# Queue order of early operands, loads from POOL's queue and a pause of preparing steps around the gate/up stage of a hybrid block

## The chip, the cores and the metric

The kernel runs on one core of a Trainium2 chip: TensorE (PE) for matrix products, VectorE (DVE), ScalarE (ACT), GpSimd (POOL), and SyncE (SP), which here only issues DMAs. The metric is device microseconds of one execution, smaller is better; the time given is the median of several runs.

## The reference

One layer on `x` of shape (1, 2048, 1024), all in float32. The part behind the two mixers is what matters here:

```python
mixed = jnp.concatenate([rmsnorm(y_ssm, norm_ssm_out_g[l]),
                         rmsnorm(y_att, norm_att_out_g[l])], axis=-1)
x = x + mixed @ w_out[l]
h2 = rmsnorm(x, norm_ffn_g[l])
x = x + (jax.nn.silu(h2 @ w_gate[l]) * (h2 @ w_up[l])) @ w_down[l]
...
return rmsnorm(x, norm_final_g)
```

The hidden width of the feed-forward part is `D_FF` = 2816. Ahead of it stand an input projection, a diagonal state-space mixer and chunked attention, which this change doesn't touch.

## The kernel before

**Products.** A float32 operand is split in two parts of a shorter type: `split` (L173 to L175) has ACT cast the high part and DVE subtract it from the value, which leaves the low part. `mm3` (L167, its matmuls on L79) makes three matmuls of each product: high times high, high times low, low times high. Nearly everything that PE does behind the attention reads such pairs, so each operand needs a DMA, an ACT cast and a DVE subtract first.

**Stages.** After the mixers (to about 900 us) comes the output projection: `w_out(sb, b, i)` for four blocks of 512 tokens and four pairs of 128-row tiles each. One call loads two tiles of `x` (`xt`, L1214), makes the products into the two-bank PSUM tile `big`, adds (L1222), stores the result as `x1` (L1223), squares it in place on ACT (L1228) and adds the squares into `sa` (L1229, L1230). The square writes where the store reads, so it waits until the store has landed. `xt` has two buffers.

Gate and up (`gate_up_phase`, about 922 to 1771 us) and down (`down_phase`, about 1771 to 2185 us) use a scheme with seven products in place of eight for a two-by-two block product; the seven are called B11, B21, T2, T1, T3, B22, T4 (numbers 0 to 6), and each reads sums or differences of blocks that were prepared before. A tail of norms and of the last tokens ends the program.

**Gate and up.** Two halves `hf` of the tokens, eleven blocks `f` of hidden rows in each, and for every block one `Proj` for gate and one for up. `one` makes B11 and T1, `two` makes T2, B21 and T3, and `three`, which is called inside the next `Proj`, makes B22 (into bank `Y`), adds, and makes T4 (into bank `X`). `product` splits the weights (`c`); the token operands of a half are seven pairs of tiles `hi`/`lo` of 1 MB each, loaded from `hc` and split by `build` (L1457). `EARLY` lists the five of them that are loaded while the output projection still runs, in the order B11, T1, T2, B21, T3; `LATE` holds B22 and T4:

```python
B11, B21, T2, T1, T3, B22, T4 = range(7)
EARLY, LATE = (B11, T1, T2, B21, T3), (B22, T4)
```

So `EARLY[:3]` are the tiles `lo0`, `lo3`, `lo2`, and `EARLY[3:]` are `lo1` and `lo4`. The first half's operands go as four loads each, the second half's as one load of 1 MB each. Between the `Proj`s, `next(pre, None)` takes one step of a generator: first the second half's token sums (`pre_steps`), then the down weights' sums (`weight_steps`, DVE adds on L1382 to L1390, results stored as `wc`).

**Down.** Hidden blocks in groups of three or two (`group`). A group makes the seven products in the order B11, T1, T2, B22, T3, B21, T4, each with an operand of hidden values from `hq` and one of weights from `wc`. `operand` takes a tile `hd` from a ring of ten, loads it (L1619) and splits it; for the first group, `early` has the loads issued by POOL, and those of B11 and T1 are issued at high priority. The results are added from PSUM (`ps`) into `acc` (L1653), which `load_acc` (L1658) fills from `x1` by 32 loads of 256 KB for the first group of each half.

**Order.** The program is given to a framework that fixes the order of each engine's instructions when the kernel is built: it takes them by priority (program order, or ahead of it inside `tc.high_priority()`), and by when it reckons that their inputs are ready. PE's order is kept as it is written. `tc.issue_after(ins)` makes what is issued inside it stand behind `ins` on the same engine. Each engine then runs its instructions strictly in that order. SP's DMAs take eight semaphores in turn, so a DMA is issued only when the one eight places before it has landed.

Of the kernel before, what the change touches and what calls it, by code (L numbers as in the profile page):

```python
# [12 lines left out]
AF = mybir.ActivationFunctionType  # L13
# [3 lines left out]
P = 128  # L17
# [80 lines left out]
def f32(ap):  # L98
    return ap.bitcast(F32)
# [73 lines left out]
def split(k, hi, lo, raw):  # L173
    nc = k.nc
    return nc.scalar.copy(hi, raw), nc.vector.tensor_tensor(lo, raw, f32(hi), op=ALU.subtract)  # L175
# [896 lines left out]
def mix_phase(k, S, bank):  # L1072
# [3 lines left out]
    with ExitStack() as cx:  # L1076
# [130 lines left out]
        def w_out(sb, b, i):  # L1207
            ts = slice(sb * SB, (sb + 1) * SB)
            if i == 0:
                b.sa = k.t(k.mf, "sa", [P, SB], bufs=2)  # L1210
            rows = slice(i * P, (i + 2) * P)
            xt = k.t(wr, "xt", [P, 1024], bufs=2)
            xv = xt[:].rearrange("p (q t) -> p q t", q=2)
            nc.sync.dma_start(xv, io["xt"][rows, ts].rearrange("(q p) t -> p q t", p=P))  # L1214
# [7 lines left out]
            nc.vector.tensor_tensor(xt[:], xt[:], ps[:], op=ALU.add)  # L1222
            nc.sync.dma_start(S["x1"][rows, ts].rearrange("(q p) t -> p q t", p=P), xv)  # L1223
            if i == 0:
                nc.scalar.activation(b.sa[:], xt[:, :512], AF.Square)
                nc.scalar.activation(xt[:, 512:], xt[:, 512:], AF.Square)
            else:
                nc.scalar.activation(xt[:], xt[:], AF.Square)  # L1228
                nc.vector.tensor_tensor(b.sa[:], b.sa[:], xt[:, :512], op=ALU.add)  # L1229
            nc.vector.tensor_tensor(b.sa[:], b.sa[:], xt[:, 512:], op=ALU.add)  # L1230
            yield

        def next_block(sb):
# [66 lines left out]
        for sb in range(NSB):  # L1300
            if sb:
                b.m = {}
                mixed(b, 0)
            if sb == 0:
                held = [w_out(0, b, 2 * n) for n in range(3)]
                next(held[0])
                next(held[1])
                ps = big()
                spread(k, te, ps[:, :512], b.o[1], 0)
                with tc.high_priority():  # L1310
                    rstd2(b, 1, ps[:, :512])
                    mixed(b, 1)
                next(held[2])
            else:
                mixed(b, 1)
            for n in range(4):
                if n == 0 and 0 < sb < NSB - 1:
                    nxt = next_block(sb + 1)
                if sb or n > 2:
                    for _ in w_out(sb, b, 2 * n):  # L1320
                        pass
                else:
                    next(held[n])
                if n in (0, 1) and xr:
                    next(xr)
                if n in (1, 2) and sb + 1 < NSB:
                    norm(nxt, n - 1)
                for _ in range(PRE0.get((sb, n), 0)):
                    next(pre)
                if (sb, n) == (NSB - 1, 1):  # L1330
                    rx.close()
                    k.ga1 = tc.alloc_tile_pool(name="ga1", reuse_waits="tile", bufs=1, side="right")
                    k.gr = tc.alloc_tile_pool(name="gr", reuse_waits="tile", bufs=2, side="right")
                    wr = cx.enter_context(tc.tile_pool(name="wr2", reuse_waits="tile", bufs=2, side="right"))
                    k.hT = build(k, S, 0, k.ga1, EARLY)
# [114 lines left out]
def build(k, S, hf, pool, ns):  # L1450

    hT = {}
    for n in ns:
        hi, lo = hT[n] = tuple(k.t(pool, f"{m}{n}", [P, 4, 512], F32R) for m in ("hi", "lo"))
        with k.tc.high_priority():
            for q in range(4) if hf == 0 else (slice(0, 4),):
                k.nc.sync.dma_start(f32(lo[:, q]), S["hc"][hf, n, :, q])  # L1457
        for q in range(4):
            split(k, hi[:, q], lo[:, q], f32(lo[:, q]))
    return hT  # L1460


def gate_up_phase(k, S):
# [3 lines left out]
    with ExitStack() as cx:  # L1467
# [13 lines left out]
        class Proj:  # L1481
# [49 lines left out]
                u3 = self.keep(self.x)  # L1531
                self.add(u3, self.y, 1, 1)

            def three(self):
                self.product(B22, self.s4, self.y, False)
                self.add(self.u2, self.y, 0, 1)
                self.product(T4, self.a22, self.x, False)
                self.post(self.x, 1, 0)

        before = None  # L1540
# [2 lines left out]
        for hf in range(2):  # L1543
            hT = build(k, S, 1, k.ga1, EARLY) if hf else k.hT
            hT.update(build(k, S, hf, ga, LATE))
            for f in range(F2):
                gs = {}

                def gt():
                    return k.t(gb, "g", [P, 512], bufs=GB_)  # L1550

                def gate(u, r, c, gs=gs):
                    g = gs[r, c] = gt()
                    nc.scalar.activation(g[:], u[:], AF.Silu)

                def up(u, r, c, gs=gs, hf=hf, f=f):
                    g = gs[r, c]
                    V.tensor_tensor(g[:], g[:], u[:], op=ALU.mult)
                    if hf and f + r * F2 in TAILF:
                        nc.sync.dma_start(S["h"][TAILF.index(f + r * F2), :, c * 512 : (c + 1) * 512], g[:])  # L1560
                        return

                    def put(n, b):
                        nc.sync.dma_start(S["hq"][hf, f, n], b[:])

                    if (r, c) == (0, 0):
                        put(B11, g)
                    elif (r, c) == (1, 1):
                        put(B22, g)
                    elif (r, c) == (0, 1):  # L1570
                        t1, t2 = gt(), gt()
                        V.tensor_tensor(t1[:], g[:], gs[0, 0][:], op=ALU.subtract)
                        put(T1, t1)
                        V.tensor_tensor(t2[:], gs[1, 1][:], t1[:], op=ALU.subtract)
                        put(T2, t2)
                        V.tensor_tensor(g[:], gs[1, 1][:], g[:], op=ALU.subtract)
                        put(T3, g)
                        gs["t2"] = t2
                    else:
                        put(B21, g)  # L1580
                        t4 = gt()
                        V.tensor_tensor(t4[:], g[:], gs["t2"][:], op=ALU.subtract)
                        put(T4, t4)

                for w, post in (("w_gate", gate), ("w_up", up)):
                    p = Proj(hT, io[w], f, post)
                    p.one()
                    if before:
                        before.three()
                    p.two()  # L1590
                    before = p
                    if hf or f > 1:
                        next(pre, None)
                if hf == 0 and f < 2:
                    next(xr)
        before.three()
    k.gr.release()
    k.ga1.release()

# [1 line left out]
def down_phase(k, S):  # L1601
    tc, nc, io = k.tc, k.nc, k.io
    V, te = nc.vector, k.te
    with ExitStack() as cx:
# [5 lines left out]
        def bank(pool):  # L1610
            return k.t(pool, "ps", [P, 512])

        def operand(src, early=False, aside=False):

            g, n = src.shape[0], src.shape[2]
            t = k.t(next(ring), "hd", [P, 2 * DG * 512], F32R)
            hi, lo = (t[:, m * g * n : (m + 1) * g * n].rearrange("p (g c) -> p g c", g=g) for m in range(2))
            with tc.high_priority() if early else ExitStack():
                (nc.gpsimd if aside else nc.sync).dma_start(f32(lo), src.rearrange("g p c -> p g c"))  # L1619
            split(k, hi, lo, f32(lo))  # L1620
            return hi, lo

        def group(hf, f0, g, acc, early):
# [6 lines left out]
            def load(m):  # L1630
                if m < len(order):
                    n = order[m][0]
                    soon = early and n in (B11, T1)
                    ops[n] = operand(S["hq"][hf, fs, n], soon, early), operand(S["wc"][fs, n], soon, early)

            if f0 == 0:
                acc += [k.t((a0, a1)[hf], f"acc{i}", [P, HALF]) for i in range(KT)]
# [241 lines left out]
```

## Time and profile before

| what | value |
|---|---|
| time, median of 3 runs | 2221.88 us (2221.82 to 2222.04) |
| profiled execution | 2217.26 us, span 2215.1 us |
| granted TensorE clock, mean | 0.992 |
| PE busy | 2153.9 us (97%) |
| DVE busy | 1534.0 us (69%) |
| ACT busy | 1009.9 us (46%) |
| POOL busy | 372.8 us (17%) |
| DMA | 431.20 MB, mean 195 GB/s |

Times in the rows below are microseconds from the start of the span. A row of the time line gives start, busy time, engine, line, operation, output and input, how many instructions stand in it, and in brackets how long the engine had idled before it and what it had waited for. A row of waits gives the total, how often, and the longest. A row of a stretch gives its bounds and length, the busy time of PE, of PE's weight loads, DVE, ACT and POOL, then the granted clock of PE, the share of the DMA engines in use and GB/s. A row of DMA issues ends with KB each and the median us from issue to landing.

### The profile page before, as it was taken

Reading aid. Unit: us, or ns where it says so; the run is one execution under the profiler, and the core shown is the slowest. Engines: PE = TensorE matmul, PEld = TensorE weight load, DVE = VectorE, ACT = ScalarE, POOL = GpSimd, SP = SyncE. Lnnn points to the kernel's source line nnn. Section 1 sums busy time; section 2 is a strip of 40 time slices with the busy share of each in tenths; the row PEclk is TensorE's granted clock in tenths of the full one; section 3 lists DMA queues with packets and bytes.
Section 4 is the critical chain, followed back from the end, with each engine's and each line's share of the span. In section 5 each row is a group of like instructions: output and inputs, shape, how many; then the busy total and the mean of one; then the engine's idle time right before and its main releaser. Section 6 shows DMA issues by size and latency. Waiting matters only on the chain.

```text
span 2215.1 us, 30093 instructions
## 1 busy us (share of the span) xinstructions
PE 2153.9 (97%) x10606; PEld 1817.4 (82%) x10606; DVE 1534.0 (69%) x2671; ACT 1009.9 (46%) x1681; POOL 372.8 (17%) x838
## 2 busy tenths in 40 slices
PE   8988999999989999999999999999999999999998
PEld 7777798998977888788888887888888778888887
DVE  8756566565568667767776768767666477689785
ACT  6356566555586631543333335333333443354332
POOL 3357777676210000000000000000000010000000
PEclk9999999999999999999999999999999999999999
DMA  9778977665743346835655557546333395465562
GB/s 331 232 246 282 298 227 235 210 208 155 224 129 127 118 143 200 277 100 186 189 160 197 196 190 269 200 158 209 114 100 114 112 393 181 169 219 199 188 221 77
DMA packets 194503, 431.20 MB, mean 195 GB/s; under 512 B 19760, under 2 KB 37216, under 8 KB 187248
## 3 DMA queue, kind: packets, MB, share of 16 engines
q1 hardware_dynamic: 186608, 404.31, 55.2%
q0 software_dynamic: 7744, 24.97, 3.6%
q8 instruction: 83, 1.36, 0.2%
q14 instruction: 68, 0.56, 0.1%
HBM read 290.00 MB, written 131.10 MB: 190 GB/s over the span
## 4 chain that ended last, share of the span: by engine, by line
PE 82%; DVE 8%; DMA 6%; issue 3%; ACT 2%; SPq 0%; POOL 0%; ACTq 0%; DVEq 0%
PE X L79 20%; PE ps L79 19%; PE pf L79 10%; PE Y L79 10%; PE big L79 6%; PE W L79 5%; PE pj L79 5%; PE pt L82 2%; PE sc L79 2%; DMA lo<-hc 1%; DMA hd<-wc 1%; DMA x<-xt 1%; DVE lo L175 1%; DMA xt<-in_xt 1%; DVE ptl L955 1%
## 5 line engine op out<-in xcount | busy, mean ns | idle before, releaser
L79 PE MATMUL X<-hi,c 128*128 128x512 f32 x1408 | 450.3, 390 | 7.6 <-DVE xt L1222 3.5
L79 PE MATMUL ps<-hd,hd 128*128 128x512 f32 (+1 forms) x1920 | 428.7, 384 | 2.6 <-DVE hd L175 2.0
L79 PEld LDWEIGHTS ps<-hd,hd 128*128 128x128 f32 x1920 | 353.2, 188 | 74.4 <-DVE hd L175 2.7
L79 PEld LDWEIGHTS X<-hi,c 128*128 128x128 f32 x1408 | 264.7, 188 | 64.4 <-DVE c L175 4.6
L79 PE MATMUL X<-lo,c 128*128 128x512 f32 x704 | 274.4, 390 | 0.0
L175 ACT CAST hd<-hd 128x1536 fp32r<-128x1536 f32 (+1 forms) x106 | 147.5, 1394 | 229.8 <-DMA hd<-hq 171.9
L79 PE MATMUL Y<-hi,c 128*128 128x512 f32 x704 | 224.5, 389 | 2.3 <-DVE u L1515 2.3
L175 DVE TENSOR_TENSOR hd<-hd 128x1536 fp32r<-128x1536 f32 (+1 forms) x106 | 174.3, 1646 | 37.0 <-ACT hd L175 36.4
L1619 POOL DMA_DIRECT2D hd<-hq x7 | 5.3, 757 | 1108.8 <-PE X L79 1095.0
L175 DVE TENSOR_TENSOR c<-S,c 128x512 fp32r<-128x512 f32 x176 | 121.1, 689 | 99.4 <-ACT c L175 99.1
L1511 ACT COPY u<-X 128x512 f32<-128x512 f32 x132 | 77.5, 588 | 195.0 <-PE X L79 195.0
L175 ACT CAST c<-S 128x512 fp32r<-128x512 f32 x176 | 109.5, 622 | 121.1 <-PE Y L79 61.6
L79 PE MATMUL big<-m,woh 128*128 128x512 f32 x512 | 161.3, 397 | 0.0
L79 PEld LDWEIGHTS Y<-hi,c 128*128 128x128 f32 x704 | 132.1, 188 | 30.6 <-DVE u L1515 3.2
L1653 DVE TENSOR_TENSOR acc<-acc,ps 128x512 f32<-128x512 f32 x196 | 130.5, 685 | 37.7 <-PE ps L79 37.3
L79 PEld LDWEIGHTS X<-lo,c 128*128 128x128 f32 x704 | 132.6, 188 | 27.5
L175 ACT CAST c<-raw 128x512 fp32r<-128x512 f32 x132 | 82.2, 623 | 148.1 <-PE Y L79 70.6
L79 PE MATMUL pf<-hi,w 128*128 128x512 f32 x416 | 147.7, 407 | 0.6 <-ACT hi L806 0.6
L79 PE MATMUL Y<-lo,c 128*128 128x512 f32 x352 | 137.0, 389 | 0.0
L955 DVE TENSOR_TENSOR ptl<-pt,pth 128x640 fp32r<-128x640 f32 (+3 forms) x152 | 98.2, 646 | 46.0 <-ACT pth L954 43.9
L938 ACT ACTIVATE s<-s,mn 128x640 f32<-128x640 f32 (+4 forms) x128 | 97.9, 765 | 53.6 <-DVE mn L935 52.0
L954 ACT CAST pth<-pt 128x640 fp32r<-128x640 f32 (+3 forms) x152 | 83.8, 551 | 77.0 <-PE pt L82 72.6
(479 smaller groups left out, 4293.6 us busy)
## 6 DMA issues: line engine op xcount, KB each, us to landing
w<-wss SPq DMA_DIRECT2D x36, 1024.0 KB, 6.0
hq<-g SPq DMA_DIRECT2D x140, 256.0 KB, 2.1
hd<-hq SPq DMA_DIRECT2D x35, 768.0 KB, 4.4
hd<-wc SPq DMA_DIRECT2D x35, 768.0 KB, 6.0
raw<-in_w_gate SPq DMA_DIRECT2D x44, 512.0 KB, 3.6
raw<-in_w_up SPq DMA_DIRECT2D x44, 512.0 KB, 4.1
wc<-px SPq DMA_DIRECT2D x66, 256.0 KB, 3.0
wss<-w SPq DMA_DIRECT2D x12, 1024.0 KB, 6.1
```

Source lines behind the costliest of these rows:

```text
L79: return self.tc.keep_in_program_order(self.tc.nc.tensor.matmul(*a, **b))
L82: return self.tc.keep_in_program_order(self.tc.nc.tensor.transpose(*a, **b))
L175: return nc.scalar.copy(hi, raw), nc.vector.tensor_tensor(lo, raw, f32(hi), op=ALU.subtract)
L938: nc.scalar.activation(s[:, :nk], s[:, :nk], AF.Exp, bias=mn[:], scale=-1.0, accum_out=sums[sb, pr][:, hh, qp : qp + 1])
L954: nc.scalar.copy(pth[:, a:b, qp, :], pt[:, a:b, :])
L955: nc.vector.tensor_tensor(ptl[:, a:b, qp, :], pt[:, a:b, :], f32(pth[:, a:b, qp, :]), op=ALU.subtract)
L1511: nc.scalar.copy(u[:], ps[:])
L1619: (nc.gpsimd if aside else nc.sync).dma_start(f32(lo), src.rearrange("g p c -> p g c"))
L1653: V.tensor_tensor(a, a, ps[:], op=ALU.add)
```

## The change

Six edits in four places:

1. `w_out` notes its last store, square and sum in `k.marks`. `build` for the first half is called twice: with `EARLY[:3]` as before, and with `EARLY[3:]` inside `issue_after` for those three marks. Eight loads (`lo1`, `lo4`) on SP, their casts on ACT and their subtracts on DVE come to stand behind the store, square and sum of the output projection's tile that was the latest at that point.
2. The second half's seven operand loads are issued by POOL, not by SP.
3. The last `Proj` makes T4 ahead of B22 (`three(True)`).
4. No step of the preparing generator is taken at the first half's last block and at the second half's first block (four calls of `next` fewer there).
5. The first down group's B11 operands are split, too, at high priority (`ahead`).
6. As a consequence of the new order, ACT loads its table for the square root (L1754, now L1768) ahead of the last `Silu`, and two more table loads follow.

```diff
-            nc.sync.dma_start(S["x1"][rows, ts].rearrange("(q p) t -> p q t", p=P), xv)
+            put = nc.sync.dma_start(S["x1"][rows, ts].rearrange("(q p) t -> p q t", p=P), xv)
...
-                nc.scalar.activation(xt[:], xt[:], AF.Square)
+                sq = nc.scalar.activation(xt[:], xt[:], AF.Square)
...
-            nc.vector.tensor_tensor(b.sa[:], b.sa[:], xt[:, 512:], op=ALU.add)
+            sa = nc.vector.tensor_tensor(b.sa[:], b.sa[:], xt[:, 512:], op=ALU.add)
+            k.marks = put, sq, sa
...
-                    k.hT = build(k, S, 0, k.ga1, EARLY)
+                    k.hT = build(k, S, 0, k.ga1, EARLY[:3])
+                    with ExitStack() as behind:
+                        for ins in k.marks:
+                            behind.enter_context(tc.issue_after(ins.ins))
+                        k.hT.update(build(k, S, 0, k.ga1, EARLY[3:]))
...
-                k.nc.sync.dma_start(f32(lo[:, q]), S["hc"][hf, n, :, q])
+                (k.nc.gpsimd if hf else k.nc.sync).dma_start(f32(lo[:, q]), S["hc"][hf, n, :, q])
...
-            def three(self):
+            def fourth(self):
+                self.product(T4, self.a22, self.x, False)
+
+            def three(self, last=False):
+                if last:
+                    self.fourth()
                 self.product(B22, self.s4, self.y, False)
                 self.add(self.u2, self.y, 0, 1)
-                self.product(T4, self.a22, self.x, False)
+                if not last:
+                    self.fourth()
                 self.post(self.x, 1, 0)
...
-                    if hf or f > 1:
+                    if 1 < hf * F2 + f not in (F2 - 1, F2):
                         next(pre, None)
...
-        before.three()
+        before.three(True)
...
-        def operand(src, early=False, aside=False):
+        def operand(src, early=False, aside=False, ahead=False):
...
-            split(k, hi, lo, f32(lo))
+                if ahead:
+                    split(k, hi, lo, f32(lo))
+            if not ahead:
+                split(k, hi, lo, f32(lo))
...
-                    ops[n] = operand(S["hq"][hf, fs, n], soon, early), operand(S["wc"][fs, n], soon, early)
+                    ops[n] = tuple(operand(src, soon, early, early and n == B11) for src in (S["hq"][hf, fs, n], S["wc"][fs, n]))
```

**Entry of gate/up, DVE.** `xt_10130` and `xt_10186` are the last two pairs of tiles of the output projection, `xt_9981` the pair before; `lo_…` are token operands, `c_10308` the first weight pair that PE reads in gate/up. Before:

```order
L175 TENSOR_TENSOR lo_2046_10061<-lo_2046_10061,hi_2045_10060 128x512
L1229 TENSOR_TENSOR sa_9863<-sa_9863,xt_9981 128x512
L1230 TENSOR_TENSOR sa_9863<-sa_9863,xt_9981 128x512
L1222 TENSOR_TENSOR xt_10130<-xt_10130,big_10132 128x1024
L1222 TENSOR_TENSOR xt_10186<-xt_10186,big_10188 128x1024
L1493 TENSOR_TENSOR S_10298<-raw_10295 128x512
L175 TENSOR_TENSOR c_10308<-raw_10294,c_10308 128x512
```

Now:

```order
L175 TENSOR_TENSOR lo_2054_10117<-lo_2054_10117,hi_2053_10116 128x512
L1222 TENSOR_TENSOR xt_10130<-xt_10130,big_10132 128x1024
L1229 TENSOR_TENSOR sa_9863<-sa_9863,xt_10130 128x512
L1222 TENSOR_TENSOR xt_10186<-xt_10186,big_10188 128x1024
L1230 TENSOR_TENSOR sa_9863<-sa_9863,xt_10130 128x512
L1498 TENSOR_TENSOR S_10298<-raw_10295 128x512
L175 TENSOR_TENSOR c_10308<-raw_10294,c_10308 128x512
```

The two sums of `xt_9981` have moved up ahead of eight of the subtracts (not shown), and the two sums of `xt_10130` have moved up to stand between the last two L1222 and ahead of `c_10308`.

**End of the first down group, ACT.** `hd_17254` and `hd_17258` are the hidden and the weight operand of the first group's T4, its last product; `hd_17354` and `hd_17358` are those of the second group's first product. Before:

```order
L175 CAST hd_17210<-hd_17210 128x1536
L175 CAST hd_17254<-hd_17254 128x1536
L175 CAST hd_17258<-hd_17258 128x1536
L175 CAST hd_17354<-hd_17354 128x1536
L175 CAST hd_17358<-hd_17358 128x1536
```

Now:

```order
L175 CAST hd_17210<-hd_17210 128x1536
L175 CAST hd_17254<-hd_17254 128x1536
L175 CAST hd_17354<-hd_17354 128x1536
L175 CAST hd_17258<-hd_17258 128x1536
L175 CAST hd_17358<-hd_17358 128x1536
```

`hd_17354` and `hd_17258` have changed places. On DVE, the two subtracts keep their order, with one `acc` sum (of `ps_17065`) between them. Before:

```order
L175 TENSOR_TENSOR hd_17258<-hd_17258 128x1536
L1653 TENSOR_TENSOR acc_3148_16984<-acc_3148_16984,ps_17064 128x512
L175 TENSOR_TENSOR hd_17354<-hd_17354 128x1536
L1653 TENSOR_TENSOR acc_3149_16985<-acc_3149_16985,ps_17065 128x512
L175 TENSOR_TENSOR hd_17358<-hd_17358 128x1536
```

Now:

```order
L1667 TENSOR_TENSOR acc_3148_16984<-acc_3148_16984,ps_17064 128x512
L175 TENSOR_TENSOR hd_17258<-hd_17258 128x1536
L1667 TENSOR_TENSOR acc_3149_16985<-acc_3149_16985,ps_17065 128x512
L175 TENSOR_TENSOR hd_17354<-hd_17354 128x1536
L1667 TENSOR_TENSOR acc_3150_16986<-acc_3150_16986,ps_16978 128x512
```

Each `acc` sum has moved one place up against the subtracts.

**Tail, DVE.** `no_19761` is the result of a norm's root, which PE transposes next; `acc_3278` and `acc_3279` are rows of the sum of the last but one block of tokens. Before:

```order
L131 TENSOR_TENSOR nf_19759<-nf_19759,nv_19758 128x4
L132 SCALAR_TENSOR_TENSOR no_19761<-nf_19759,ny_19760 128x4
L1669 TENSOR_TENSOR acc_3278_18364<-acc_3278_18364,ps_19768 128x256
L1669 TENSOR_TENSOR acc_3279_18365<-acc_3279_18365,ps_19769 128x256
L1687 TENSOR_TENSOR sb_19742<-sb_19742,sg_19795 128x256
```

Now:

```order
L131 TENSOR_TENSOR nf_19759<-nf_19759,nv_19758 128x4
L1683 TENSOR_TENSOR acc_3278_18364<-acc_3278_18364,ps_19768 128x256
L132 SCALAR_TENSOR_TENSOR no_19761<-nf_19759,ny_19760 128x4
L1683 TENSOR_TENSOR acc_3279_18365<-acc_3279_18365,ps_19769 128x256
L1701 TENSOR_TENSOR sb_19742<-sb_19742,sg_19795 128x256
```

One `acc` sum has moved ahead of `no`. PE's own order differs in one place only: the last two products of gate/up.

More of the change, by code (lines that the diff above doesn't have):

```diff
@@ L1222, in w_out @@
             nc.vector.tensor_tensor(xt[:], xt[:], ps[:], op=ALU.add)
-            nc.sync.dma_start(S["x1"][rows, ts].rearrange("(q p) t -> p q t", p=P), xv)
+            put = nc.sync.dma_start(S["x1"][rows, ts].rearrange("(q p) t -> p q t", p=P), xv)
             if i == 0:
                 nc.scalar.activation(b.sa[:], xt[:, :512], AF.Square)
-                nc.scalar.activation(xt[:, 512:], xt[:, 512:], AF.Square)
+                sq = nc.scalar.activation(xt[:, 512:], xt[:, 512:], AF.Square)
             else:
-                nc.scalar.activation(xt[:], xt[:], AF.Square)
+                sq = nc.scalar.activation(xt[:], xt[:], AF.Square)
                 nc.vector.tensor_tensor(b.sa[:], b.sa[:], xt[:, :512], op=ALU.add)
-            nc.vector.tensor_tensor(b.sa[:], b.sa[:], xt[:, 512:], op=ALU.add)
+            sa = nc.vector.tensor_tensor(b.sa[:], b.sa[:], xt[:, 512:], op=ALU.add)
+            k.marks = put, sq, sa
             yield
```

## The prediction

> **What bounds the kernel now.** I read the page first, then PE's waits, then the time lines around each wait.
>
> ```profile
> span 2215.1 us, 30093 instructions
> PE 2153.9 (97%) x10606; PEld 1817.4 (82%) x10606; DVE 1534.0 (69%) x2671; ACT 1009.9 (46%) x1681; POOL 372.8 (17%) x838
> PE 82%; DVE 8%; DMA 6%; issue 3%; ACT 2%; SPq 0%; POOL 0%; ACTq 0%; DVEq 0%
> ```
>
> PE is busy for 2153.9 of 2215.1 us, and the change adds and removes no product. Time can only move in PE's 61 us of idle time, and in the clock after it. PE's waits behind the attention are few:
>
> ```profile
> PE X L79 <- DVE xt L1222: 3.5, 1, 3.5
> PE X L79 <- DVE c L175: 3.4, 1, 3.4
> PE Y L79 <- DVE u L1515: 2.3, 2, 1.5
> PE ps L79 <- DVE hd L175: 2.0, 2, 1.8
> ```
>
> They lie at three seams: entry of gate/up (3.5), switch to its second half (3.4), entry of the down stage (1.5 and 1.8). So 10 us is the most that this change could take away; everything else it does is a risk of new waits. The measurement can tell about 0.2% from no change, here 4.4 us.
>
> **The change part by part.** *Entry of gate/up* (twelve early loads, then the stores and sums of the last `w_out` tiles, then eight loads).
>
> ```profile
> 891.64 14.95 SPq L1457 DMA_DIRECT2D lo<-hc  x20
> 907.02 0.37 SPq L1223 DMA_DIRECT2D x<-xt  x1
> 912.86 1.06 ACT L1228 ACTIVATE xt<-xt 128x1024 f32<-128x1024 f32 x1 [0.81 <-DVE lo L175]
> 913.96 0.69 DVE L1229 TENSOR_TENSOR sa<-sa,xt 128x512 f32<-128x512 f32 x1 [1.18 <-ACT xt L1228]
> 915.45 0.90 SPq L1214 DMA_DIRECT2D xt<-in_xt  x2
> 919.81 2.45 DVE L1222 TENSOR_TENSOR xt<-xt,big 128x1024 f32<-128x1024 f32 x2 [4.43 <-DMA xt<-in_xt]
> 922.40 0.70 PE L79 MATMUL X<-hi,c 128*128 128x512 f32 x1 [3.54 <-DVE xt L1222]
> 922.77 0.69 DVE L175 TENSOR_TENSOR c<-raw,c 128x512 fp32r<-128x512 f32 x1
> 924.64 1.06 ACT L1228 ACTIVATE xt<-xt 128x1024 f32<-128x1024 f32 x1 [1.13 <-DMA x<-xt]
> ```
>
> SP takes 14.95 us for twenty loads, 0.75 each, and only then issues the store at 907.02. With eight loads behind it, it goes out 8 x 0.75 = 6.0 us earlier. The square (in place, so behind the store's landing), the sums and the two `xt` loads at 915.45 follow, so these loads leave at about 909.3. As long a flight as before (915.45 to 919.81, 4.36 us) and eight more loads in the same queues bring the first L1222 to 914 or 915, some 5 us earlier than 919.81. But the two L1222 no longer stand together on DVE: a sum L1229 is between them, and it waits for a square that waits for the first tile's store. Before, that store left at the end of the first L1222 (half of 2.45, so 921.04) and the square began at 924.64, 3.6 us later. From the first L1222 to the end of the second it now takes 1.22 + 3.6 + 1.09 (square and hand-over, 912.86 to 913.96 gives 1.10) + 0.6 + 1.22 = 7.8 us. The second ends at 921.8 to 922.8, where it ended at 922.26. Then L1230 stands ahead of the first `c`, 0.6 us more for the third matmul. I take +0.4. Below: the first L1222 at 912.5 gives -1.5; above: 2.5 us of further delay by the eight loads gives +3.
>
> *Second half's loads* (seven of 1 MB from POOL's queue), with four steps of preparation fewer at the switch.
>
> ```profile
> 1334.85 3.04 SPq L1457 DMA_DIRECT2D lo<-hc  x2
> 1339.70 0.62 ACT L175 CAST hi<-lo 128x512 fp32r<-128x512 f32 x1 [1.23 <-DMA lo<-hc]
> 1340.80 1.29 DVE L175 TENSOR_TENSOR lo<-lo,hi 128x512 fp32r<-128x512 f32 x2
> 1364.40 0.72 PE L79 MATMUL X<-hi,c 128*128 128x512 f32 x2 [3.44 <-DVE c L175]
> 1340.00:1360.00 20.00, 19.34 (x86) 15.67 (x85) 20.00 (x34) 15.07 (x30) 0.00 (x0) 1.00 1.00 358
> lo<-hc SPq DMA_DIRECT2D x7, 1024.0 KB, 5.0
> hd<-hq POOLq DMA_DIRECT2D x1, 768.0 KB, 4.4
> ```
>
> DVE is busy for 20.00 of 20 us here, and PE's 3.44 us are what DVE is late. The pause takes three weight sums of 0.6 us out of it, 1.8 us. But the operand `lo2` was loaded at 1334.85 and its cast waited for the landing until 1339.70: the first subtract could be only 0.48 earlier (1340.32 for 1340.80). A POOL load took 4.4 us for 768 KB, 5.0 is SP's median for 1 MB: an estimate for POOL is 4.4 to 5.9 (in proportion). I take -0.2, between -1.2 (all three sums saved on a later path) and +1.5 (the slow landing and a new ACT order). The four steps find room later: of 40 calls (two for each of twenty blocks) 36 remain, for 32 steps.
>
> [...]
>
> *Entry of the down stage* (last T4 ahead of B22, split of the first operands at high priority).
>
> ```profile
> 1764.19 0.59 ACT L1511 COPY u<-X 128x512 f32<-128x512 f32 x1 [4.85 <-PE X L79]
> 1772.20 3.42 DVE L175 TENSOR_TENSOR hd<-hd 128x1536 fp32r<-128x1536 f32 x2
> 1774.01 26.18 PE L79 MATMUL ps<-hd,hd 128*128 128x512 f32 x114 [1.76 <-DVE hd L175]
> ```
>
> T4 needs only the copy that ends at 1764.78, where B22 needed DVE's add (PE's wait of 1.5 for `u`): 0.7 us. DVE then has one of its two operand splits behind it before the last add, and the other ends near 1772.9, where PE waited until 1774.01: 1.1 us earlier in all. What comes next takes this back. The cast of `hd_17354`, the second group's first operand, now stands ahead of that of `hd_17258`, the first group's last.
>
> ```profile
> 1804.25 1.48 ACT L175 CAST hd<-hd 128x1536 fp32r<-128x1536 f32 x1 [1.56 <-DMA hd<-wc]
> 1805.77 1.76 DVE L175 TENSOR_TENSOR hd<-hd 128x1536 fp32r<-128x1536 f32 x1 [0.69 <-ACT hd L175]
> 1807.41 0.37 SPq L1619 DMA_DIRECT2D hd<-hq  x1
> 1813.86 1.48 ACT L175 CAST hd<-hd 128x1536 fp32r<-128x1536 f32 x1 [8.13 <-DMA hd<-hq]
> 1815.38 1.76 DVE L175 TENSOR_TENSOR hd<-hd 128x1536 fp32r<-128x1536 f32 x1 [7.26 <-ACT hd L175]
> 1817.05 0.68 DVE L1653 TENSOR_TENSOR acc<-acc,ps 128x512 f32<-128x512 f32 x1
> 1830.17 1.89 DVE L1653 TENSOR_TENSOR acc<-acc,ps 128x512 f32<-128x512 f32 x3
> 1831.60 14.75 PE L79 MATMUL ps<-hd,hd 128*128 128x512 f32 x64 [0.59 <-DVE acc L1653]
> 1810.00:1815.00 5.00, 5.00 (x24) 4.14 (x23) 0.00 (x0) 1.14 (x1) 0.00 (x0) 1.00 1.05 405
> ```
>
> `hd_17258` was there at 1804.25. `hd_17354` was issued at 1807.41, behind 32 loads of `acc`, with the DMA engines full (share 1.05), and cast at 1813.86 after 8.13 us of idling. Now `hd_17258` waits for it: its cast runs 1815.34 to 1816.82, its subtract from 1816.86. DVE idled 7.26 us before 1815.38 and is back to back after it, up to the second of the three sums at 1830.17, for which PE waited (the three end at 1832.06, the second 0.6 before, 1831.45): 16.07 us of work. This work now starts 1.48 later and holds one split more (1.67 from start to start, 1815.38 to 1817.05), so it ends at 1816.86 + 1.67 + 16.07 = 1834.60, and PE gets its bank at 1834.75 for 1831.60: **+3.15** at this place. The earlier entry is no part of it, since the landing sets it. PE stopped at 1831.60 - 0.59 = 1831.01; now at 1829.9 it idles 4.9 us. I keep the landing as it was, as its DMA engines were full; 1.5 us either way, so +1.6 to +4.6.
>
> *The clock after such a gap.*
>
> ```profile
> 922.00:926.00 4.00, 3.60 (x8) 2.46 (x9) 3.54 (x7) 1.98 (x3) 0.00 (x0) 0.57 1.02 281
> 1364.00:1368.00 4.00, 3.60 (x16) 2.97 (x17) 3.35 (x6) 0.98 (x2) 0.00 (x0) 1.00 0.24 62
> ```
>
> After 3.54 us of idling PE ran 4 us at a mean clock of 0.57, after 3.44 us at 1.00. A gap of 4.9 us is beyond both. The price is (1 - 0.57) x 4 = 1.7 at most; without the 0.4 us in which PE still idled there it is about 1.3. I take +1.3, between 0 and 1.7. [...]
>
> *The tail.*
>
> ```profile
> 2188.19 0.16 DVE L132 SCALAR_TENSOR_TENSOR no<-nf,ny 128x4 f32<-128x4 f32 x1
> 2189.26 0.78 DVE L1669 TENSOR_TENSOR acc<-acc,ps 128x256 f32<-128x256 f32 x2 [0.91 <-PE ps L79]
> 2189.42 0.60 PE L82 MATMUL ps<-ident,no 128*128 128x128 f32 x4
> ```
>
> One sum of 0.4 us, which waits for PE until 2189.26, now stands ahead of `no`, which the transposes at 2189.42 need: `no` is done at 2189.26 + 0.42 + 0.16, with the hand-over 2189.9, so +0.5 (0 to 0.6).
>
> **Sum:** 0.4 - 0.2 + 3.15 + 1.3 + 0.5 = +5.1. The profiled execution took 2217.26 us (span 2215.1), so it would take 2222.4; the runs' median stands 4.6 higher, and gives 2221.88 + 5.1 = 2227.0.
>
> **The rivals.** *Late cast, full clock.* Everything as above, but the gap falls as at 1364.40 and the clock stays 1.00: 5.1 - 1.3 = +3.8, 2225.7, within 0.2%.
>
> *The late cast finds cover: not slower.* If `hd_17354` is cast by 1809.2, DVE's chain ends at 1809.2 + 4.67 + 16.07 = 1829.9, when PE ends, and only the entry's -1.1 is left: 0.4 - 0.2 - 1.1 + 0.5 = -0.4, 2221.5. Two stores of `h` between the `acc` loads swap places on SP, so these loads may leave without a pause. Against it: 4.7 us are wanted, and a queue that is served by full engines empties no sooner for being filled sooner.
>
> *All seams close.* If the eight loads cost nothing and landings at the first seam get quicker by 2 us each, PE starts at 918.9 and its wait of 3.5 with 0.8 of the cold clock goes (-4.3); with -1.2 at the switch and -1.1 at the down stage, this is -6 with the tail, 2215.9. Against it speaks the 3.6 us landing between the two L1222.
>
> *POOL's loads land late.* PE's wait at the switch is DVE's lateness, so each us by which `lo2` lands later than now is a us. With landings of 8 instead of 5 us it is +3 on top: +8, 2229.9. [...]
>
> **How the numbers follow.** The late cast follows from the fixed orders of ACT and DVE, so I give it 0.40 with the cold clock and 0.27 without; the cover 0.15; all seams 0.08; late POOL loads 0.10. Predicted: 2227.0. The range 2221.0 to 2230.5 takes in the first two, most of the cover and the POOL case, and leaves out the closing of all seams and the worst ends together. Within 0.2% (2217.4 to 2226.3) lie the full clock and the cover, 0.42; slower the forecast and the POOL case, 0.50; faster 0.08.
>
> **What would show it.** In the changed kernel's trace: PE waits 4 to 5 us for `acc` near 1834 with a clock near 0.5 behind it; ACT has two casts of `hd` back to back from about 1813.9; at the first seam one sum between the two L1222 with DVE idle ahead of it for 3 us; PE's wait at the switch stays 3 to 4 us; down's first long run of matmuls starts a us earlier. It is wrong if `hd_17354` is cast before 1810, if the second L1222 ends before 920, or if PE's wait for `c` at the switch is under 2 or over 5 us.

## The result, and the profile after

The changed kernel takes 2230.87 us (median of 5 runs, 2230.12 to 2235.38) against 2221.88 us (5 runs, 2220.11 to 2224.73): a ratio of 1.0040, 95% interval 1.0029 to 1.0051. It is 9.0 us slower, where 5.1 were forecast; the median lies 0.4 us above the range. The interval of the ratio is 6.4 to 11.3 us: the forecast 5.1 lies below it, while the 0.4 us past the range's end are less than this noise.

The profiled execution took 2231.66 us, its span is 14.2 us longer than that of before. The page and PE's waits of the changed kernel:

```profile
span 2229.3 us, 30105 instructions
PE 2158.1 (97%) x10606; PEld 1819.8 (82%) x10606; DVE 1535.5 (69%) x2671; ACT 1011.2 (45%) x1683; POOL 377.2 (17%) x845
PE X L79 <- DVE c L175: 6.0, 2, 5.5
PE ps L79 <- DVE acc L1667: 4.4, 1, 4.4
PE X L79 <- DVE xt L1222: 4.1, 1, 4.1
PE ps L79 <- DVE hd L175: 2.0, 1, 2.0
```

PE has the same 10606 matmuls and is busy for 4.2 us longer with them over the whole span. From the last sums of squares to the transposes in the tail (first and last row below) 13.7 us are lost; PE's waits behind 895 us add up to 18.6 us where they were 12.5, which is 6.1 of them, and the rest is the same matmuls at a lower clock. Set beside each other at the same matmuls, PE's starts show where the time went (from the two time lines, us):

| place | before | changed | behind by |
|---|---|---|---|
| last sums of squares ahead of gate/up | 884.64 | 884.95 | 0.31 |
| first X of gate/up | 922.40 | 923.32 | 0.92 |
| a product 20 us on | 944.37 | 946.01 | 1.64 |
| switch, product that waits for `c` | 1364.40 | 1368.98 | 4.58 |
| 2.4 us on | 1366.82 | 1373.41 | 6.59 |
| first long run of down | 1774.01 | 1779.74 | 5.73 |
| second group's first bank | 1831.60 | 1842.66 | 11.06 |
| 2.8 us on | 1834.41 | 1847.92 | 13.51 |
| transposes in the tail | 2189.42 | 2203.42 | 14.00 |

The first seam, on the time lines of SP, DVE, ACT and PE:

```profile
893.00 8.00 SPq L1462 DMA_DIRECT2D lo<-hc  x12
901.85 0.37 SPq L1223 DMA_DIRECT2D x<-xt  x1
915.85 1.22 DVE L1222 TENSOR_TENSOR xt<-xt,big 128x1024 f32<-128x1024 f32 x1
920.27 1.06 ACT L1228 ACTIVATE xt<-xt 128x1024 f32<-128x1024 f32 x1 [5.17 <-DMA x<-xt]
921.35 0.69 DVE L1229 TENSOR_TENSOR sa<-sa,xt 128x512 f32<-128x512 f32 x1 [4.28 <-ACT xt L1228]
921.96 1.21 DVE L1222 TENSOR_TENSOR xt<-xt,big 128x1024 f32<-128x1024 f32 x1
923.32 0.76 PE L79 MATMUL X<-hi,c 128*128 128x512 f32 x1 [4.12 <-DVE xt L1222]
925.03 1.22 PE L79 MATMUL X<-hi,c 128*128 128x512 f32 x2 [0.52 <-DVE c L175]
```

The store leaves 5.2 us earlier than before (907.02) and the first L1222 starts 4.0 us earlier (919.81); DVE then idles 4.28 us in front of the sum between the two L1222, because ACT's square waits for the first tile's store to land, and nothing of the gain is left: the second starts at 921.96, and PE starts X 0.9 us later than before.

The switch: a stretch, DMA queues, and time lines of POOL, ACT, DVE and PE.

```profile
1340.00:1360.00 20.00, 19.34 (x84) 15.67 (x84) 17.72 (x30) 13.27 (x26) 1.59 (x3) 1.00 0.87 334
lo<-hc POOLq DMA_DIRECT2D x5, 1024.0 KB, 6.0
DMA to landing us min/median/max: 5.4/6.0/8.8
q0 software_dynamic: 205, 1.42, 38.6%
q1 hardware_dynamic: 432, 1.05, 35.4%
1343.09 0.53 POOL L1462 DMA_DIRECT2D lo<-hc  x1 [3.22 <-PE X L79]
1351.94 2.18 ACT L175 CAST hi<-lo 128x512 fp32r<-128x512 f32 x4 [1.54 <-DMA lo<-hc]
1352.60 2.50 DVE L175 TENSOR_TENSOR lo<-lo,hi 128x512 fp32r<-128x512 f32 x4 [1.54 <-ACT hi L175]
1368.98 1.22 PE L79 MATMUL X<-hi,c 128*128 128x512 f32 x2 [5.46 <-DVE c L175]
```

DVE, busy for 20.00 of 20 us before, is now busy for 17.72: it waits for operands. The load that took 8.8 us is the one that POOL issued at 1343.09. ACT's cast waited for it until 1351.94 and DVE's subtract until 1352.60, and from there on DVE works without a pause up to the `c` that PE waits for. The two queue rows are of 1343 to 1352: POOL's queue (q0) moved 1.42 MB there while SP's (q1) moved 1.05 MB. When SP issued these loads, they stood ahead of SP's own stores.

The down stage, on the time lines of ACT, DVE and PE, and the clock in three stretches:

```profile
1779.74 58.54 PE L79 MATMUL ps<-hd,hd 128*128 128x512 f32 x250 [2.00 <-DVE hd L175]
1812.42 1.48 ACT L175 CAST hd<-hd 128x1536 fp32r<-128x1536 f32 x1 [2.23 <-DMA hd<-hq]
1821.88 7.16 ACT L175 CAST hd<-hd 128x1536 fp32r<-128x1536 f32 x5 [7.98 <-DMA hd<-hq]
1824.77 1.76 DVE L175 TENSOR_TENSOR hd<-hd 128x1536 fp32r<-128x1536 f32 x1 [8.48 <-ACT hd L175]
1842.66 7.56 PE L79 MATMUL ps<-hd,hd 128*128 128x512 f32 x21 [4.37 <-DVE acc L1667]
1366.00:1374.00 8.00, 5.02 (x13) 3.98 (x14) 5.33 (x9) 2.15 (x4) 0.00 (x0) 0.57 0.19 66
1779.00:1783.00 4.00, 3.26 (x8) 2.58 (x9) 2.96 (x3) 0.00 (x0) 2.07 (x3) 0.60 1.02 375
1840.00:1848.00 8.00, 5.34 (x13) 4.21 (x14) 8.00 (x9) 2.94 (x2) 0.00 (x0) 0.58 0.51 190
```

The casts of `hd` run back to back from 1821.88, where `hd_17354` has landed; DVE begins 2.89 us after that, behind two casts, and is late for PE by 4.37. PE ran at half clock after each of the four waits. The trace's clock record, of which the stretches are means, shows half clock from 923.04, 1366.77 and 1841.22 for 6.83 us each and from 1779.78 for 3.41 us; in the trace of before it shows 3.41 us, once, between 900 us and the end of PE's work.

### The profile page after: what moved, and what is told of

Read it like the earlier page. It is cut to its first block, busy times and chain, and to the rows that moved or that the text cites. A ratio compares the mean times of both kernels' runs of the same rounds, so it can differ in the third digit from the quotient of the medians.

```text
span 2229.3 us, 30105 instructions
## 1 busy us (share of the span) xinstructions
PE 2158.1 (97%) x10606; PEld 1819.8 (82%) x10606; DVE 1535.5 (69%) x2671; ACT 1011.2 (45%) x1683; POOL 377.2 (17%) x845
## 4 chain that ended last, share of the span: by engine, by line
PE 81%; DMA 7%; DVE 7%; issue 2%; ACT 2%; SPq 0%; ACTq 0%; DVEq 0%; POOL 0%; POOLq 0%
PE X L79 21%; PE ps L79 19%; PE Y L79 10%; PE pf L79 10%; PE big L79 6%; PE W L79 5%; PE pj L79 4%; PE pt L82 2%; PE sc L79 2%; DMA acc<-x 2%; DMA lo<-hc 1%; DMA x<-xt 1%; DMA xt<-in_xt 1%; DVE ptl L955 1%; DMA xt<-in_xp 1%
```

## The experiments

Each was timed in five rounds beside the kernel before on the same chip. The runs of the kernel before spread there from 2216.1 to 2230.7 us with medians of 2222.6 to 2223.8, so the ratios carry the verdicts, and the profiles the places. The split of the first down operands at high priority was not run alone.

**T4 ahead of B22, alone**

```diff
-        before.three()
+        before.three(True)
```

> The kernel before with one edit: the last Proj makes T4 ahead of B22. The cast of hd_17354 then stands ahead of that of hd_17258 as in the changed kernel. Theory (the late cast costs): PE's entry to the down stage 0.9 us earlier, then a wait of 4 to 5 us for acc at the second group's first bank (0.59 before), one or two half-clock windows behind it, 0.5 us in the tail; median 4 to 6 us over the kernel before. Rival (the late landing of hd_17354 that the changed kernel shows comes from the other edits, and the order of casts has cover): wait under 1 us there, median within 1 us of the kernel before.

Ratio 1.0028 (1.0019 to 1.0038); median 2228.82 for 2223.51, as the theory expected.

**The same with the casts in the old order**

```diff
+            first_last = getattr(k, "split", None) if (hf, f0) == (0, DG) else None
...
-                split(k, hi, lo, f32(lo))
+                with ExitStack() as behind:
+                    if k.after:
+                        for ins in k.after:
+                            behind.enter_context(tc.issue_after(ins.ins))
+                    k.split = split(k, hi, lo, f32(lo))
```

> As the run with T4 alone, with one pair of instructions exchanged: hd_17258 is cast ahead of hd_17354 again, nothing else on any engine differs. Theory: PE's wait at the second group's first bank falls to under 1 us, no half-clock window there; what is left of T4 is the entry's -0.9 and the tail's +0.5, so the median is 0 to 1 us under the kernel before. Rival (the wait comes from the later landing, whatever the order): still 4 us of wait, and the median as with T4 alone.

Ratio 0.9994 (0.9984 to 1.0004); median 2221.92 for 2223.51. Time lines of ACT and PE, first with T4 alone:

```profile
1820.21 5.60 ACT L175 CAST hd<-hd 128x1536 fp32r<-128x1536 f32 x4 [9.28 <-DMA hd<-hq]
1825.50 10.76 PE L79 MATMUL ps<-hd,hd 128*128 128x512 f32 x45 [1.95 <-DVE acc L1663]
1840.99 1.44 PE L79 MATMUL ps<-hd,hd 128*128 128x512 f32 x3 [4.72 <-DVE acc L1663]
```

then with the old order of casts:

```profile
1820.39 1.48 ACT L175 CAST hd<-hd 128x1536 fp32r<-128x1536 f32 x1 [5.99 <-DMA hd<-hq]
1837.53 1.86 PE L79 MATMUL ps<-hd,hd 128*128 128x512 f32 x7 [1.45 <-DVE acc L1671]
```

`hd_17354` landed at the same time in both (1820.21 and 1820.39), and one exchanged pair of casts makes the wait 4.72 or 1.45. With T4 alone PE waits for `acc` a first time as well, 1.95 us at 1825.50, which the changed kernel's trace does not show. So the cleanest measure is not the wait but the time from the cast of `hd_17354` to PE's start at the second group's first bank:

| casts and T4 | from cast to PE's start |
|---|---|
| old order, T4 behind B22: before, and five runs below (loads from POOL, pause, marks alone, marks with the two L1222 together, late sums) | 17.74 us in all six |
| old order, T4 ahead of B22 (this run and three below) | 17.14 us in all four |
| new order: changed, T4 alone, changed with the loads back on SP | 20.78 us in two, 20.79 in one |

The time of the landing sets when the bank comes free, and the order of the two casts adds 3.64 us (20.78 for 17.14), or 3.04 against the kernel before. The prediction's sum for that pair was 3.15 (1834.75 - 1813.86 = 20.89 for 17.74). The late cast is shown, and with it the larger part of the loss. The wait kept, 1.45 us, was somewhat over the 1 us expected.

**The second half's loads from POOL, alone**

```diff
-                k.nc.sync.dma_start(f32(lo[:, q]), S["hc"][hf, n, :, q])
+                (k.nc.gpsimd if hf else k.nc.sync).dma_start(f32(lo[:, q]), S["hc"][hf, n, :, q])
```

> The kernel before with one edit: the second half's seven loads are issued by POOL. Theory (they land later): issue to landing of lo 5.5 us or more (5.0 by SP), DVE with pauses of 3 us or more between 1335 and 1360 where it had none, PE's wait for c at the switch 5 to 6 us (3.44 before) with a half-clock window or two behind it; median 2 to 4 us over the kernel before. Rival (the late landings come from the pause of the weight sums and the new order, not the queue): wait of 3 to 4 us, median within 1 us.

Ratio 1.0012 (1.0001 to 1.0023); median 2225.06 for 2223.51. The loads' landings, and PE at the switch:

```profile
DMA to landing us min/median/max: 5.2/7.4/10.1
1361.24 0.79 PE L79 MATMUL X<-hi,c 128*128 128x512 f32 x1 [2.30 <-ACT u L1512]
1370.52 0.73 PE L79 MATMUL X<-hi,c 128*128 128x512 f32 x2 [4.39 <-DVE c L175]
```

The landings took 7.4 us in the median (5.0 from SP), and the waits of 0.66 and 3.44 us became 2.30 and 4.39. The queue alone does it. The wait for `c` itself is under the 5 us expected, and the loss (1.6 us by the medians, 0.2 to 5.1 by the ratio's interval) is only just told from none.

**The pause alone**

```diff
-                    if hf or f > 1:
+                    if 1 < hf * F2 + f not in (F2 - 1, F2):
```

> The kernel before with one edit: no preparing step at the two blocks round the switch of the halves. Theory (as predicted: DVE only trades the three sums of 0.6 us for waiting on lo2's landing): PE's wait for c at the switch 2.9 to 3.4 us (3.44 before), median 0 to 1 us under the kernel before. Rival (the 1.8 us come off the wait in full): wait 1.6 us or less, so short that no half-clock window follows, median 2 to 3.5 us under it. Other rival (what was skipped comes back later as a wait in gate/up or down): median 1 us or more over it.

Ratio 0.9990 (0.9978 to 1.0003); median 2221.08 for 2222.64; PE's wait for `c` was 3.43 us, as long as before (3.44), close to what the theory has, and a gain is not told from none.

**The changed kernel with the loads back on SP**

> The changed kernel with the second half's loads given back to SP, all else as changed. Theory (POOL's late landings make the wait at the switch): PE's wait for c there 3 to 3.5 us (5.46 in the changed kernel), median 2 to 4 us under the changed kernel's 2230.9, so 2227 to 2229. Rival (the pause and the late blocks around it make the wait): it stays above 5 us, and the median at 2230 to 2232.

Ratio to the kernel before 1.0022 (1.0012 to 1.0032); median 2228.13. PE's waits at the switch and at the second group:

```profile
1370.46 0.94 PE L79 MATMUL X<-hi,c 128*128 128x512 f32 x2 [3.54 <-DVE c L175]
1843.81 1.62 PE L79 MATMUL ps<-hd,hd 128*128 128x512 f32 x3 [4.69 <-DVE acc L1667]
```

5.46 us became 3.54, and the late cast stayed, as the theory expected. The median is 2.7 us lower; as the two kernels were timed at different times, the ratios to the kernel before are the fairer measure, 1.0040 and 1.0022, and their intervals touch.

**The changed kernel with T4 back behind B22**

> The changed kernel with T4 behind B22 again, all else as changed. Theory (T4 with its late cast carries most of the loss): PE's wait at the second group's first bank under 2 us, median 4 to 6.5 us under the changed kernel's 2230.9, so 2224.5 to 2227. Rival (the parts share the loss evenly): at most 3 us under it.

Ratio 1.0008 (0.9997 to 1.0019); median 2224.14, 6.7 us under the changed kernel (0.32% by the ratios), somewhat more than expected, and PE has no wait for `acc` at the second group. T4's place carries most of the loss.

**The marks alone** (`EARLY[3:]` behind the marks, as in the change)

> The kernel before with one edit: lo1 and lo4 stand behind the marks. Theory (the sum L1229 between the two L1222 eats what the earlier loads gain): the first L1222 3 to 5 us earlier than before, 5 to 6 us from its start to that of the second, PE's wait before X 3.5 to 4.5 us, 0.5 us more ahead of the third matmul; median 0.5 to 2 us over the kernel before. Rival (the earlier loads win): wait under 2.5 us, median 1 us or more under it.

Ratio 1.0006 (0.9992 to 1.0020). In its profile PE waited 4.65 us before X, just over the 3.5 to 4.5 expected, but the time does not differ measurably from that of the kernel before.

**Marks with the two L1222 together and early first splits**

```diff
+            added = nc.vector.tensor_tensor(xt[:], xt[:], ps[:], op=ALU.add)
+            if (sb, i) == (NSB - 1, 6):
+                with tc.issue_after(added.ins):
+                    k.held()
...
+                with tc.high_priority() if self.soon and n in (B11, T1) else ExitStack():
+                    split(k, c[:, 0], c[:, 1], raw)
```

> lo1 and lo4 behind the marks, as in the run with the marks alone, and two things more: the sums of the last but one pair of tiles are issued behind the last L1222, and the first Proj's first two splits at high priority, so that on DVE the two L1222 and the first c are together. Theory (the sum between the two L1222 eats the gain of the earlier loads): the last L1222 ends near 918.5, PE's wait before X falls from 4.7 to under 1.5 us, no half-clock window there; median 3 to 5 us under the kernel before. Rival (another input of the first products, the eight later loads or the splits, is late next): a new wait of over 2 us before 945, median within 1.5 us of the kernel before.

Ratio 1.0002 (0.9991 to 1.0013). Time lines of DVE, ACT and PE:

```profile
917.63 1.22 DVE L1222 TENSOR_TENSOR xt<-xt,big 128x1024 f32<-128x1024 f32 x1 [0.83 <-PE big L79]
920.20 1.06 ACT L1231 ACTIVATE xt<-xt 128x1024 f32<-128x1024 f32 x1 [6.82 <-DMA x<-xt]
921.16 0.60 ACT L175 CAST c<-raw 128x512 fp32r<-128x512 f32 x1
921.82 0.79 PE L79 MATMUL X<-hi,c 128*128 128x512 f32 x1 [4.22 <-ACT c L175]
```

The last L1222 ends at 918.85, as the theory has it, but the cast of `c` stands on ACT behind the square of the pair before, for whose store ACT waits 6.82 us: the wait only changed its name. The rival holds.

**A first combined kernel** (marks and early splits as in the last run, pause, T4 with the old order of casts, split at high priority, loads by SP)

> What the runs so far let stand, in one kernel: marks with the two L1222 together and the early first splits, pause, T4 ahead of B22 with hd_17258 cast ahead of hd_17354, split at high priority, loads by SP. Theory (the parts add up): -3 to -5 from the first seam, -0.5 from the switch, -1 to 0 from the down stage; median 3.5 to 6.5 us under the kernel before. Rival (the seams are coupled by the DMA queue and a gain at the first comes back as a wait at the second group's first bank): a wait of 2 to 3 us there and a median at most 2 us under it.

Ratio 0.9996 (0.9985 to 1.0007): no gain that can be told. PE still waited 2.02 us for ACT's cast of `c` at the first seam and 3.5 us at the switch; its wait at the second group was 0.7 us, so the rival's place was wrong, too.

**Late sums S.** What the profile of the switch offered: DVE made three sums ahead of the `c` that PE waited for, and only later products read them.

```diff
...
+                def rest():
+                    self.s2 = s(self.s1, self.a11, ALU.subtract)
+                    self.s3 = s(self.a11, a21, ALU.subtract)
+                    self.s4 = s(self.a12, self.s2, ALU.subtract)
...
-                self.s2 = s(self.s1, self.a11, ALU.subtract)
-                self.s3 = s(self.a11, a21, ALU.subtract)
-                self.s4 = s(self.a12, self.s2, ALU.subtract)
...
+                if f:
+                    rest()
...
                     p.one()
+                    if f == 0:
+                        p.rest()
```

> The kernel before with one edit that the change does not have: for the first block of each half the three sums S (L1493) that only the later products need are made behind the splits of the first two products. At the switch DVE then has c ahead of three sums of 0.6 us. Theory (PE's 3.44 us there are DVE's lateness alone, and a gap that fills little more than half of a 3.41 us clock window costs a half-clock window too): PE's wait for c at the switch 1.6 to 1.8 us, no half-clock window behind it; median 2 to 4 us under the kernel before. Rival (PE waits for a copy or for an operand lo next): wait still over 2.5 us, median within 1 us.

Ratio 0.9983 (0.9974 to 0.9993); median 2219.19 for 2222.78. PE at the switch, the clock behind it, and PE at the second group:

```profile
1363.90 0.73 PE L79 MATMUL X<-hi,c 128*128 128x512 f32 x2 [1.54 <-DVE c L175]
1363.00:1367.00 4.00, 3.10 (x14) 2.56 (x15) 4.00 (x8) 1.79 (x5) 0.00 (x0) 1.00 0.61 211
1834.20 2.31 PE L79 MATMUL ps<-hd,hd 128*128 128x512 f32 x5 [3.04 <-DVE acc L1670]
```

3.44 us became 1.54, with full clock behind it: 0.17% faster than the kernel before, by an edit that the change didn't have. In this profile part of it comes back as 3.04 us at the second group's first bank, 17.74 us behind the cast of `hd_17354` as in the kernel before.

**A second combined kernel** (the first with the late sums in place of the early splits, and the square and sums of `xt_10130` on POOL)

```diff
+                if aside:
+                    nc.gpsimd.tensor_tensor(xt[:], xt[:], xt[:], op=ALU.mult)
```

> The combined kernel with two things more: the late sums S of the run beside it, in place of the high priority of the first splits; and the square and the two sums of the last but one pair of tiles on POOL, so that neither ACT nor DVE waits for that pair's store ahead of the first c. Theory (in the first combined kernel ACT's in-place square held up the cast of c at the first seam): PE's wait before X under 1 us and the wait for c at the switch 1.2 to 1.8 us, no half-clock window at either; median 5 to 8 us under the kernel before. Rival (the next input is late at once, as in the two runs before): a wait of 2 us or more in the first products or at T2, median at most 3 us under it.

Ratio 0.9980 (0.9971 to 0.9988); median 2219.24 for 2222.78. No better than the late sums alone can be told, and short of the 5 us expected. Time lines of DVE, POOL and PE:

```profile
924.88 1.85 DVE L1506 TENSOR_TENSOR S<-raw 128x512 f32<-128x512 f32 x1
926.65 1.75 DVE L175 TENSOR_TENSOR c<-raw,c 128x512 fp32r<-128x512 f32 x1
930.01 0.68 DVE L175 TENSOR_TENSOR c<-S,c 128x512 fp32r<-128x512 f32 x1
924.29 1.89 POOL L1230 TENSOR_TENSOR xt<-xt 128x1024 f32<-128x1024 f32 x1 [267.80 <-DMA x<-xt]
926.26 1.59 POOL L1233 TENSOR_TENSOR sa<-sa,xt 128x512 f32<-128x512 f32 x1
928.46 0.80 PE L79 MATMUL X<-hi,c 128*128 128x512 f32 x1 [2.65 <-DVE c L175]
```

ACT is free of the store now, but DVE's operations took 1.75 to 1.85 us while POOL worked and 0.68 after it, and PE waited for the slow one.

**Late sums, pause, T4 with the old order of casts** (split at high priority; marks left out, loads by SP)

> The kernel before with the late sums S, the pause, T4 ahead of B22 with hd_17258 cast ahead of hd_17354, and the split of B11's operands at high priority; the eight loads unmoved, loads by SP. Theory (parts that touch different seams add up): ratios 0.9983, 0.999 and 0.9994 give 0.9967, so a median 6 to 8 us under the kernel before, with PE's wait for c at the switch under 1.6 us and no half-clock window there. Rival (the pause and the late sums take the same idle time at the switch, and cannot both count): a median 3 to 5 us under it.

Ratio 0.9983 (0.9972 to 0.9995); median 2219.79 for 2223.79. PE at the switch and at the second group:

```profile
1363.00 0.74 PE L79 MATMUL X<-hi,c 128*128 128x512 f32 x2 [1.65 <-DVE c L175]
1831.55 1.88 PE L79 MATMUL ps<-hd,hd 128*128 128x512 f32 x6 [2.81 <-DVE acc L1678]
```

The parts did not add up: 4.0 us where 6 to 8 were expected. The wait for `c` is 1.65, no shorter than with the late sums alone, which fits the rival; the 2.81 us at the second group, where the bank comes free 17.14 us behind the cast of `hd_17354`, are time gained ahead and given back. How the missing gain splits between the two was not separated.

## Why the prediction was wrong, by its own steps

- **Direction and largest term: right.** The late cast was forecast at +3.15 us with 4.9 us of idling. The trace has 4.37 us of idling, and the time from cast to bank grew by 3.04 us, or by 3.64 with T4 in the same place. T4 alone costs 0.28% (6.2 us) of the 0.40%, where the prediction's terms for it, 3.15, the clock's 1.3 and the tail's 0.5, give 4.95.
- **The switch: the step that failed.** "I take -0.2", since a POOL load "took 4.4 us for 768 KB". That row was one load with the engines to itself (a stretch in which SP's queue moved nothing). The seven loads took 5.4 to 8.8 us, the slowest of them beside 1.05 MB in SP's queue, and PE's wait went from 3.44 to 5.46. In place of -0.2 the term was about +2.7 us (0.12%) with the loads alone, and 4.0 (0.18%) when they were taken out of the changed kernel, both with wide intervals. The prediction had this as a rival at 0.10, with just this price ("landings of 8 instead of 5 us"), and a wait of over 5 us was one of its signs of being wrong. The DMA issues of the whole execution before also had a row for POOL's loads in which most of them share the engines with another queue:

```profile
hd<-hq POOLq DMA_DIRECT2D x7, 768.0 KB, 10.6
```

  For half the loads it gives more than twice the 4.4 us, for less data. It overstates this case (6.0 us in the median here), but it would have put the late loads into the forecast: with the prediction's own price 5.1 + 3 = 8.1 us, near the 9.0.
- **The clock: its fall right, size off.** This is the second term that was mis-sized. One term of +1.3 stood in the sum, at one place. The trace has half clock behind four waits, 6.83 us behind three of them. At the second group that is 2.45 us (11.06 to 13.51), at the switch 2.0, at the entry of down 1.4 (5.73 to 7.14 by 1782.88). Nor was the step of half clock behind a gap of 4.9 us open, as the chances of 0.40 and 0.27 had it: such a gap idles PE for at least 0.72 of one step of 3.41 us wherever the step begins (half of 4.9 when a step's bound halves it), and by the table at the end all 29 steps with over 0.60 were followed by half clock.
- **First seam: right in this trace.** +0.4 forecast, +0.6 at the first X; 6.1 us from L1222 to L1222 for the 6.5 that its terms give (1.22 + 3.6 + 1.09 + 0.6); 0.52 for the 0.6 of the third matmul. With the 0.52 and a second half-clock step it came to 1.3 in this execution; alone, the marks show no difference in time, with an interval of -1.8 to +4.4 us.
- **Entry of down: right as far as the wait goes.** -1.1 forecast, -0.86 measured (6.59 to 5.73). Not seen: two waits of 1.45 and 1.76 us, 6.7 us apart, became one of 2.00, and that one brought half clock here. Over all traces the difference is small: the one wait did so in four of seven, the two waits in two of seven.
- **Tail: right.** +0.5 forecast, 13.51 to 14.00 measured.
- **The base was a lucky execution.** The trace of before has one step of half clock behind 900 us although PE waits 3.44 us at the switch; of the nine traces where that wait is 3.3 to 3.6 us, seven have one right there. This is at least part of why the two traces differ by 14.2 us, the medians by 9.0.

The parts measured alone (T4, loads, marks, pause) give 0.28 + 0.12 + 0.06 - 0.10 = 0.36%, beside 0.40% (0.29 to 0.51) for the whole; the marks and the pause are not told from none, and the loads only just.

## What to carry to other kernels

Where engines run in a fixed order, an edit in one place can exchange two instructions far from it: look for the exchanged pair, and take its price from the landing that the earlier one waits for. A load that moves to another queue no longer stands ahead of the old queue's stores; price it by a row in which both queues are busy (the second half's loads alone took 7.4 us to land in the median from POOL's queue, 5.0 from SP's). When PE waits on a saturated engine, ask first which of that engine's instructions ahead of the awaited one nobody needs yet: three sums moved behind it made the only single edit here with a gain clear of the noise (0.17%). And two profiles that differ by more than the medians do should be compared with their steps of half clock counted (here seven and one between 900 us and the end of PE's work).

## What the runs showed of the hardware

**The clock.** In all 14 traces the granted clock changes in steps of 3.41 us, with one phase in a trace and another in the next. Set against PE's idle time in each step (steps from 900 to 2180 us, all traces):

```
a step at full clock, PE idle for            steps   next one at half clock
under 0.50 of it                             5143    0
0.50 to 0.56                                 5       2
0.56 to 0.60                                 7       6
over 0.60                                    29      29
a step at half clock, PE idle for
under 0.13 of it                             36      0
0.13 to 0.20                                 4       3
0.20 and more                                12      12
```

So what decides lies, in these traces, between 0.50 and 0.60 of the step idle, 1.7 to 2.0 us, and a step at half clock goes on to a second one if PE idles for more than about a seventh of it (0.13 to 0.20). One step at half clock costs at most half its length, 1.7 us (worked out from the 3.41). This is why 1.54 us of waiting was free of it and 2.00 us was not always: a wait can be split between two steps. A wait of 2.00 us (1.99 in one trace) at the entry of down was followed by half clock in four of the seven traces that have one.

**DVE beside POOL.** In the second combined kernel, three DVE operations of 128x512 with two inputs took 1.75 to 1.85 us each from 924.88 to 930.09, while POOL made its square and sums (924.29 to 929.54); the next four, from 930.01 on, took 0.68.

**Two DMA queues.** From 1343 to 1352 us of the changed kernel's trace, in which the load of 1 MB that POOL issued at 1343.09 was under way (8.8 us to landing, where SP's median before was 5.0), the packets of POOL's queue took 38.6% of the engines' time and those of SP's queue 35.4%. That this sharing alone made the load late was not shown.
